# Feed-forward stages by seven block products: another order of units and products, sums beside the hi parts, a lent raw buffer

## The chip, the cores and the metric

The kernel runs on one core of one Trainium2 chip. The metric is the device time of one execution in microseconds, the median of several runs. TensorE is the engine of the matmuls, VectorE (DVE) and ScalarE (ACT) work on tiles in SBUF and in the banks of PSUM, SyncE (SP) issues the DMAs of the weights in order, GpSimd (POOL) does little here.

## What is computed

Two transformer blocks in float32 on 512 rows of 1024 columns. Of the whole, these lines of the reference are the part that the change touches, three feed-forward stages (two SwiGLU, one with a squared ReLU):

```python
def swiglu(x, w_in, w_out):
    gate, up = jnp.split(x @ w_in, 2, axis=-1)
    return (jax.nn.silu(gate) * up) @ w_out
...
        f = rmsnorm(h, pre_ff_g[l]) @ w_ff1[l]
        f = jnp.square(jax.nn.relu(f)) @ w_ff2[l]
```

`w_in` is 1024 x 5632 (22 blocks of 128 gate columns and 22 of 128 up columns), `w_ff1` 1024 x 4096. Attention, the mixers and the second matrices of the feed-forward stages stand between and are untouched.

## The kernel before

Every float32 product is made of three matmuls: each operand is split into a hi part, rounded to the type that TensorE takes in one pass, and a lo part, the remainder; `passes` (line 281) adds hi x hi, lo x hi and hi x lo. The activations stand transposed in `xh` and `xl` (8 blocks of 128 columns x 512 rows).

The weights come through the class `Weights`. `specs` lists the loads in order, each a tile of 128 x 1024 in one of three raw buffers (pool `raw`, name `wraw`); `load` (line 66) issues the next DMA on SP's queue. `units` lists what TensorE consumes, in order; `_split` (line 106) makes of a unit a hi part (`whi`, ScalarE, line 120) and a lo part (`wlo`, VectorE, line 121) in one of five pairs of buffers. `done` (line 148) tells that TensorE has read a unit; then `fill` splits the unit five places on, and `_loads` issues loads while raw buffers are free. A raw buffer is free when its last reader, a lo part, is done.

A feed-forward stage goes over pairs of column blocks, f = 0 to 21 in the first two (gate block f and up block f), 0 to 15 in the third. Pairs that are not in `FAST` (or `FAST1`) take two ordinary units, each 24 matmuls of 512 columns. A fast pair (`Blocks.__call__`, line 485) uses the scheme of seven block products instead of eight: the two weight tiles are four blocks, a11 and a12 (first column block, upper and lower half of the 1024 inputs), a21 and a22 (second column block), and x has four blocks as well, half of the inputs times half of the rows. Seven products of sums of blocks, each of 12 matmuls of 256 columns, 84 in all, are combined to four results. The sums of x stand in `th` and `tl`, made once in a stage by `steps` (two after each of the first ordinary tiles); those of the weights are made for each pair by four vector instructions in `_source` (lines 97 to 100), in the raw tiles themselves. A fast pair has four units:

- part 0: the first raw tile as it is (a11, a12), two products with x itself;
- part 1: a22 alone, half a tile, one product with a sum of x;
- part 2: the first tile after the four sums, a product with a sum of x and one with x;
- part 3: the second tile after the sums, two products with sums of x.

The products go to the two halves of four PSUM banks a, b, c, d; line 500 (ScalarE) and lines 506, 512, 513 and 514 (VectorE) add them up to `z`, from which the stage's activation is made (lines 784 and 785 in the first two stages). `z` and its helper `u` alternate between two places, one of which is a tile of its own.

The instructions of each engine but SP are put into an order by a scheduler when the program is built; SP's stand as the program calls them. Each engine works through its own in that order.

Of the kernel before, what the change touches and what calls it, by code (L numbers as in the profile page):

```python
# [10 lines left out]
F32 = mybir.dt.float32  # L11
# [44 lines left out]
class Weights:  # L56


    def __init__(self, nc, raw, pairs, specs, units, n_raw, n_pairs):
        self.nc, self.raw, self.pairs, self.specs, self.units = nc, raw, pairs, specs, units  # L60
        self.n_raw, self.n_pairs = n_raw, n_pairs
        self.loaded, self.used, self.split, self.released = 0, 0, 0, 0
        self.r, self.p, self.extra = {}, {}, set()

    def load(self, parts=0):
        i = self.loaded
        src, (a, b), n = self.specs[i]
        t = self.raw.tile([128, 1024], F32, name="wraw")
# [5 lines left out]
        self.loaded += 1  # L74
        if parts:
# [3 lines left out]

    def _source(self, i, part):  # L80

# [4 lines left out]
        if part is None:  # L86
            self.used += 1
            return self.r.pop(i)[:, :]
        if part == 0:
            return self.r[i][:, :]  # L90
        one, two = (self.r[i + n] for n in range(2))
        (a11, a12), (a21, a22) = ((t[:, :512], t[:, 512:]) for t in (one, two))
        if part == 1:
            return a22
        if part == 2:
            tt = self.nc.vector.tensor_tensor
            tt(a22, a21, a22, op=OP.add)  # L97
            tt(a21, a11, a21, op=OP.subtract)  # L98
            tt(a11, a22, a11, op=OP.subtract)  # L99
            tt(a12, a12, a11, op=OP.subtract)  # L100
            return one[:, :]
        self.used += 2
        del self.r[i], self.r[i + 1]
        return two[:, :]

    def _split(self, pool, steps=1, name=None):
        i, part = self.units[self.split]
        t = self._source(i, part)
# [8 lines left out]
        def step(steps):  # L117
            for s in steps:
                sl = slice(s * n, (s + 1) * n)
                self.nc.scalar.activation(hi[:, sl], t[:, sl], AF.Copy)  # L120
                self.nc.vector.tensor_tensor(lo[:, sl], t[:, sl], hi[:, sl].bitcast(F32), op=OP.subtract)  # L121
# [7 lines left out]
    def _loads(self):  # L129
        while self.loaded < min(self.used + self.n_raw, len(self.specs)):  # L130
            self.load()
# [27 lines left out]
def body(ctx, tc, ins, out, stop=None, dbg=None):  # L159
# [11 lines left out]
    specs, units, at = [], [], {}  # L171
# [7 lines left out]
    def spec_pair(key, w, c0, c1, fast):  # L179
# [5 lines left out]
        for m, c in enumerate((c0, c1)):  # L185
# [62 lines left out]
    W = Weights(nc, raw, pairs, specs, units, 3, 5)  # L248
# [203 lines left out]
    class Blocks:  # L452
# [29 lines left out]
        def __call__(self, key):  # L482
# [16 lines left out]
            product(0, 0, d[:, 0], X, 0, 0)  # L499
            nc.scalar.activation(z[:, 1], d[:, 0], AF.Copy)  # L500
            product(0, 1, a[:, 0], X, 1, 0)
            W.done(at[key, 0])
            product(1, 0, c[:, 1], T, 1, 0)
            W.done(at[key, 1])
            product(2, 0, a[:, 1], T, 1, 1)
            tt(z[:, 0:4:3], a, z[:, 1:2].to_broadcast([128, 2, 256]), op=OP.add)
            product(2, 1, c[:, 0], X, 1, 1)
# [834 lines left out]
```

## Time and profile before

| what | before |
|---|---|
| runs | 1786.63, 1788.59, 1794.02 us, median 1788.59 |
| profiled execution | 1788.74 us, its span 1787.0 us |
| TensorE busy (matmuls) | 1739.1 us, 97% |
| weight loads of TensorE busy | 1532.7 us, 86% |
| VectorE busy | 1184.7 us, 66% |
| ScalarE busy | 865.3 us, 48% |
| moved by DMA | 176.83 MB, 99 GB/s |

The span is the time from the first to the last instruction; the execution's own time is a little longer. Busy time of matmuls counts each from its start to its modelled end, and they overlap, so that it says little of what TensorE loses; starts do.

### The profile page before, as it was taken

Reading aid. Unit: us, or ns where it says so; the run is one execution under the profiler, and the core shown is the slowest. Engines: PE = TensorE matmul, PEld = TensorE weight load, DVE = VectorE, ACT = ScalarE, POOL = GpSimd, SP = SyncE. Lnnn points to the kernel's source line nnn. Section 1 sums busy time; section 2 is a strip of 40 time slices with the busy share of each in tenths; the row PEclk is TensorE's granted clock in tenths of the full one; section 3 lists DMA queues with packets and bytes.
Section 4 is the critical chain, followed back from the end, with each engine's and each line's share of the span. In section 5 each row is a group of like instructions: output and inputs, shape, how many; then the busy total and the mean of one; then the engine's idle time right before and its main releaser. Section 6 shows DMA issues by size and latency. Waiting matters only on the chain.

```text
span 1787.0 us, 26502 instructions
## 1 busy us (share of the span) xinstructions
PE 1739.1 (97%) x10496; PEld 1532.7 (86%) x10496; DVE 1184.7 (66%) x2028; ACT 865.3 (48%) x1470; POOL 70.9 (4%) x125
## 2 busy tenths in 40 slices
PE   8899999999999999999999999999999999999998
PEld 8788879899988888888899998888877899988886
DVE  6888856788764467777778878447456587773333
ACT  6878833334343258878443334233434444552232
POOL 0000002000000010000000000001101100000000
PEclk9999999999999999999999999999999999999999
DMA  6221236243353142322324244441322222343331
GB/s 204 59 60 60 83 100 196 76 114 95 95 171 124 48 125 83 90 83 71 107 60 114 78 116 124 137 131 48 96 82 77 83 83 82 108 142 107 100 100 47
DMA packets 198235, 176.83 MB, mean 99 GB/s; under 512 B 7008, under 2 KB 175136, under 8 KB 198112
## 3 DMA queue, kind: packets, MB, share of 16 engines
q1 hardware_dynamic: 194384, 162.48, 30.6%
q0 software_dynamic: 3152, 10.84, 2.1%
q8 instruction: 82, 1.34, 0.3%
q10 hardware_dynamic: 576, 1.84, 0.3%
q14 instruction: 41, 0.34, 0.1%
HBM read 172.99 MB, written 7.38 MB: 101 GB/s over the span
## 4 chain that ended last, share of the span: by engine, by line
PE 71%; DVE 12%; ACT 8%; DMA 6%; issue 2%; POOL 0%; ACTq 0%; SPq 0%; DVEq 0%; POOLq 0%
PE ps L286 35%; PE ps L372 30%; DMA wraw<-in_ffn_w_in 4%; ACT whi L120 4%; DVE wlo L121 3%; DMA wraw<-in_w_ff 1%; PE ps L302 1%; DVE wraw L100 1%; DVE wraw L98 1%; DVE wraw L99 1%; PE ps L884 1%; DVE wraw L97 1%; PE ps L872 1%; ACT x L616 1%; PE ps L571 1%
## 5 line engine op out<-in xcount | busy, mean ns | idle before, releaser
L120 ACT ACTIVATE whi<-wraw 128x1024 fp32r<-128x1024 f32 (+2 forms) x356 | 348.7, 1000 | 398.3 <-DVE wraw L100 133.6
L121 DVE TENSOR_TENSOR wlo<-wraw,whi 128x1024 fp32r<-128x1024 f32 (+2 forms) x356 | 405.4, 1155 | 189.1 <-ACT whi L120 187.0
L286 PE MATMUL ps<-xh,whi 128*128 128x256 f32 (+1 forms) x1260 | 406.6, 324 | 1.0 <-ACT xh L304 1.0
L286 PE MATMUL ps<-xl,whi 128*128 128x256 f32 (+1 forms) x1260 | 405.3, 322 | 0.5 <-DVE xl L305 0.3
L286 PE MATMUL ps<-xh,wlo 128*128 128x256 f32 (+1 forms) x1260 | 405.5, 322 | 0.0
L286 PEld LDWEIGHTS ps<-xh,whi 128*128 128x128 f32 x1260 | 238.5, 190 | 18.9 <-ACT xh L304 2.4
L286 PEld LDWEIGHTS ps<-xl,whi 128*128 128x128 f32 x1260 | 239.5, 190 | 17.2 <-DVE xl L305 1.0
L286 PEld LDWEIGHTS ps<-xh,wlo 128*128 128x128 f32 x1260 | 239.4, 190 | 17.2
L286 PE MATMUL ps<-th,wlo 128*128 128x256 f32 x624 | 175.0, 280 | 9.6 <-DVE wlo L121 9.4
L286 PE MATMUL ps<-th,whi 128*128 128x256 f32 x624 | 174.8, 280 | 8.3 <-ACT whi L120 8.3
L372 PE MATMUL ps<-whi,sh 128*128 128x512 f32 x568 | 175.8, 390 | 0.0
L372 PE MATMUL ps<-wlo,sh 128*128 128x512 f32 x568 | 175.6, 389 | 0.0
L372 PE MATMUL ps<-whi,sl 128*128 128x512 f32 x568 | 175.5, 389 | 0.0
L286 PE MATMUL ps<-tl,whi 128*128 128x256 f32 x624 | 173.3, 278 | 0.0
L754 DVE TENSOR_TENSOR sl<-h,sh 128x512 fp32r<-128x512 f32 x76 | 51.6, 691 | 175.5 <-ACT sh L753 175.5
L753 ACT ACTIVATE sh<-h 128x512 fp32r<-128x512 f32 x76 | 46.7, 628 | 212.9 <-PE ps L372 189.7
L286 PEld LDWEIGHTS ps<-th,wlo 128*128 128x128 f32 x624 | 117.8, 189 | 12.9 <-DVE wlo L121 12.8
L286 PEld LDWEIGHTS ps<-th,whi 128*128 128x128 f32 x624 | 117.9, 189 | 10.5 <-ACT whi L120 10.5
L286 PE MATMUL ps<-whi,xh 128*128 128x256 f32 (+1 forms) x384 | 125.8, 328 | 0.0
L372 PEld LDWEIGHTS ps<-whi,sl 128*128 128x128 f32 x568 | 106.6, 188 | 22.2
L372 PEld LDWEIGHTS ps<-wlo,sh 128*128 128x128 f32 x568 | 106.6, 188 | 22.2
L372 PEld LDWEIGHTS ps<-whi,sh 128*128 128x128 f32 x568 | 106.3, 188 | 21.8
(323 smaller groups left out, 2800.9 us busy)
## 6 DMA issues: line engine op xcount, KB each, us to landing
wraw<-in_ffn_w_in SPq DMA_DIRECT2D x88, 512.0 KB, 4.9
wraw<-in_w_ff SPq DMA_DIRECT2D x64, 512.0 KB, 4.0
wraw<-in_ffn_w_out SPq DMA_DIRECT2D x44, 512.0 KB, 3.5
wraw<-in_a_w_qkv SPq DMA_DIRECT2D x23, 512.0 KB, 4.0
wraw<-in_w_in SPq DMA_DIRECT2D x20, 512.0 KB, 3.7
wraw<-in_kv_w SPq DMA_DIRECT2D x16, 512.0 KB, 3.9
copies<-extd POOLq DMA_DIRECT2D x16, 320.0 KB, 8.5
wraw<-in_a_w_o SPq DMA_DIRECT2D x8, 512.0 KB, 3.5
```

The lines of the kernel that those rows point to most:

```text
L97: tt(a22, a21, a22, op=OP.add)
L98: tt(a21, a11, a21, op=OP.subtract)
L99: tt(a11, a22, a11, op=OP.subtract)
L100: tt(a12, a12, a11, op=OP.subtract)
L120: self.nc.scalar.activation(hi[:, sl], t[:, sl], AF.Copy)
L121: self.nc.vector.tensor_tensor(lo[:, sl], t[:, sl], hi[:, sl].bitcast(F32), op=OP.subtract)
L286: nc.tensor.matmul(ps, lhs[a][lsel], rhs[b][rsel], start=first and n == 0, stop=last and n == 2)
L302: nc.tensor.transpose(p[:, k, :], y[:, ts(4 * c + k)], ident)
L372: nc.tensor.matmul(self.banks[t][c], act[a][:, ts(t)], w[b][:, 0, c * 512:(c + 1) * 512], start=first and n == 0, stop=last and n == 2)
L571: yield lambda: nc.tensor.matmul(p[:, :N], part[m][:, ts(i)], part[2 + m][:, :N], start=True, stop=False)
L753: nc.scalar.activation(hi, src[k], AF.Copy)
L754: nc.vector.tensor_tensor(lo, src[k], hi.bitcast(F32), op=OP.subtract)
```

## The change

The two tiles of a fast pair are loaded in the other order, the second column block first. The units are: part 0 a22 alone; part 1 the other tile as it is; part 2 the tile of a21 and a22 after the first two sums; part 3 the tile of a11 and a12 after the other two, which are issued between the hi and the lo part of part 2 (`more`). The products follow the units. The raw tile of the second block is given back at part 2, that of the first at part 3. A set `lent` names loads, from f = 7 on, whose place in the list is divisible by four: they go into a tile that the stage lends (`room`, or the second `y` tile in the third stage) and that counts apart from the three raw buffers. The second `z` now lies in a free half of a tile of the stage.

```diff
--- before.py
+++ after.py
@@ -56,56 +56,62 @@
 class Weights:
 
 
-    def __init__(self, nc, raw, pairs, specs, units, n_raw, n_pairs):
-        self.nc, self.raw, self.pairs, self.specs, self.units = nc, raw, pairs, specs, units
-        self.n_raw, self.n_pairs = n_raw, n_pairs
-        self.loaded, self.used, self.split, self.released = 0, 0, 0, 0
+    def __init__(self, nc, raw, pairs, specs, units, lent, n_raw, n_pairs):
+        self.nc, self.raw, self.pairs, self.specs, self.units, self.lent = nc, raw, pairs, specs, units, lent
+        self.room, self.n_pairs, self.lender = [n_raw, 1], n_pairs, None
+        self.loaded, self.split, self.released = 0, 0, 0
         self.r, self.p, self.extra = {}, {}, set()
 
     def load(self, parts=0):
         i = self.loaded
         src, (a, b), n = self.specs[i]
-        t = self.raw.tile([128, 1024], F32, name="wraw")
+
+        t = self.lender() if i in self.lent else self.raw.tile([128, 1024], F32, name="wraw")
         v = t[:, :a * b].rearrange("p (a b) -> p a b", a=a)
         if n is not None:
             self.nc.gpsimd.memset(t[:, :a * b], 0.0)
             v = v[:, :, :n]
         self.r[i] = t
         self.loaded += 1
+        self.room[i in self.lent] -= 1
         if parts:
             part = lambda a, m: a[:, m * a.shape[1] // parts:(m + 1) * a.shape[1] // parts]
             return lambda m: self.nc.sync.dma_start(part(v, m), part(src, m))
         self.nc.sync.dma_start(v, src)
 
+    def _used(self, i):
+        self.room[i in self.lent] += 1
+        return self.r.pop(i)
+
     def _source(self, i, part):
+
 
 
 
         while self.loaded <= i + (part not in (None, 0)):
             self.load()
         if part is None:
-            self.used += 1
-            return self.r.pop(i)[:, :]
+            return self._used(i)[:, :], None
         if part == 0:
-            return self.r[i][:, :]
-        one, two = (self.r[i + n] for n in range(2))
-        (a11, a12), (a21, a22) = ((t[:, :512], t[:, 512:]) for t in (one, two))
+            return self.r[i][:, 512:], None
         if part == 1:
-            return a22
-        if part == 2:
-            tt = self.nc.vector.tensor_tensor
-            tt(a22, a21, a22, op=OP.add)
-            tt(a21, a11, a21, op=OP.subtract)
+            return self.r[i + 1][:, :], None
+        if part == 3:
+            return self._used(i + 1)[:, :], None
+        (a11, a12), (a21, a22) = ((t[:, :512], t[:, 512:]) for t in (self.r[i + 1], self.r[i]))
+        tt = self.nc.vector.tensor_tensor
+        tt(a22, a21, a22, op=OP.add)
+        tt(a21, a11, a21, op=OP.subtract)
+
+        def more():
             tt(a11, a22, a11, op=OP.subtract)
             tt(a12, a12, a11, op=OP.subtract)
-            return one[:, :]
-        self.used += 2
-        del self.r[i], self.r[i + 1]
-        return two[:, :]
+
+        return self._used(i)[:, :], more
 
     def _split(self, pool, steps=1, name=None):
         i, part = self.units[self.split]
-        t = self._source(i, part)
+        t, between = self._source(i, part)
         (a, b) = (t.shape[1] // 128, 128) if part is not None else self.specs[i][1]
         if name:
             both = pool.tile([128, 2048], F32, name=name).bitcast(F32R)
@@ -118,6 +124,8 @@
             for s in steps:
                 sl = slice(s * n, (s + 1) * n)
                 self.nc.scalar.activation(hi[:, sl], t[:, sl], AF.Copy)
+                if between:
+                    between()
                 self.nc.vector.tensor_tensor(lo[:, sl], t[:, sl], hi[:, sl].bitcast(F32), op=OP.subtract)
 
         step(range((steps + 1) // 2))
@@ -127,7 +135,7 @@
         return rest
 
     def _loads(self):
-        while self.loaded < min(self.used + self.n_raw, len(self.specs)):
+        while self.loaded < len(self.specs) and self.room[self.loaded in self.lent]:
             self.load()
 
     def ahead(self, pool, n, name=None):
@@ -168,7 +176,7 @@
         return bass.AP(tensor=w.tensor, offset=w.offset + r0 * ld + c0, ap=[[ld, 128], [128 * ld, nk], [1, n]])
 
 
-    specs, units, at = [], [], {}
+    specs, units, lent, at = [], [], set(), {}
 
     def spec(key, w, r0, nk, c0, n, pad=None, unit=True):
         if unit:
@@ -182,7 +190,9 @@
             for part in range(4):
                 at[key, part] = len(units)
                 units.append((len(specs), part))
-        for m, c in enumerate((c0, c1)):
+        for m, c in ((1, c1), (0, c0)) if fast else ((0, c0), (1, c1)):
+            if fast and key[-1] >= 7 and len(specs) % 4 == 0:
+                lent.add(len(specs))
             spec((key, "one", m), w, 0, 8, c, 128, unit=not fast)
 
     def rows(key, w, n):
@@ -245,7 +255,7 @@
     x = [const.tile([128, D], F32, name=f"x{t}") for t in range(NT)]
     xh = const.tile([128, KT, S], F32R, name="xh")
     xl = const.tile([128, KT, S], F32R, name="xl")
-    W = Weights(nc, raw, pairs, specs, units, 3, 5)
+    W = Weights(nc, raw, pairs, specs, units, lent, 3, 5)
 
     def load_x(t):
         nc.sync.dma_start(x[t], ins["x"][0, ts(t), :])
@@ -496,22 +506,22 @@
                            (*sel, slice(256 * right, 256 * right + 256)))
 
             X, T, tt = (xh, xl), self.t, nc.vector.tensor_tensor
-            product(0, 0, d[:, 0], X, 0, 0)
+            product(0, 0, c[:, 1], T, 1, 0)
+            W.done(at[key, 0])
+            product(1, 0, d[:, 0], X, 0, 0)
             nc.scalar.activation(z[:, 1], d[:, 0], AF.Copy)
-            product(0, 1, a[:, 0], X, 1, 0)
-            W.done(at[key, 0])
-            product(1, 0, c[:, 1], T, 1, 0)
+            product(1, 1, a[:, 0], X, 1, 0)
             W.done(at[key, 1])
-            product(2, 0, a[:, 1], T, 1, 1)
+            product(2, 0, b[:, 1], T, 0, 1)
+            product(2, 1, b[:, 0], T, 0, 0)
+            W.done(at[key, 2])
+            product(3, 0, a[:, 1], T, 1, 1)
             tt(z[:, 0:4:3], a, z[:, 1:2].to_broadcast([128, 2, 256]), op=OP.add)
-            product(2, 1, c[:, 0], X, 1, 1)
-            W.done(at[key, 2])
-            product(3, 0, b[:, 1], T, 0, 1)
-            product(3, 1, b[:, 0], T, 0, 0)
+            tt(u, b, z[:, 3:4].to_broadcast([128, 2, 256]), op=OP.add)
+            tt(z[:, 3], b[:, 0], u[:, 1], op=OP.add)
+            product(3, 1, c[:, 0], X, 1, 1)
             W.done(at[key, 3])
-            tt(u, b, z[:, 3:4].to_broadcast([128, 2, 256]), op=OP.add)
             tt(z[:, 1:3], c, u, op=OP.add)
-            tt(z[:, 3], b[:, 0], u[:, 1], op=OP.add)
             return z
 
     def part_project(key, state, part):
@@ -770,7 +780,9 @@
                 th, tl = (bp.tile([128, PAD + 8 * S], F32R, name=n)[:, PAD:].rearrange("p (j k s) -> p j k s", j=2, k=4)
                           for n, PAD in (("th", 112), ("tl", 0)))
                 blocks = Blocks([t.rearrange("p (k s) -> p k s", k=4) for t in four[4:6]], th, tl,
-                                lambda: bp.tile([128, 2 * S], F32, name="z"))
+                                lambda: four[5][:, 2 * S:])
+                room = bp.tile([128, 2 * S], F32, name="room")
+                W.lender = lambda: room
 
                 def evac(n, p):
                     f = n // 2
@@ -1279,6 +1291,14 @@
     with tc.tile_pool(name="blocks2", bufs=1) as bp:
         th, tl = (bp.tile([128, PAD + 8 * S], F32R, name=n)[:, PAD:].rearrange("p (j k s) -> p j k s", j=2, k=4)
                   for n, PAD in (("th2", 112), ("tl2", 0)))
+        room = []
+
+        def lender():
+            if not room:
+                room.append(yp.tile([128, D], F32, name="y"))
+            return room[0]
+
+        W.lender = lender
         blocks = Blocks([h[:, 14:18], h[:, 18:22]], th, tl, lambda: yp.tile([128, D], F32, name="y"))
         in_tiles(f1(0, 14), evac_f1, 5,
                  [[], [lambda: after_mix(2)], [], [], [lambda: after_mix(3)]], fast_f1, side_steps(blocks.steps(), 0, 2))
```

How the order of the instructions moves is seen at two places; line numbers are those of each kernel's own text. The first is VectorE in the first feed-forward stage, one round of the queue between fast pairs. L121 (now L129) makes a lo part, L97 to L100 (now L103, L104, L107, L108) the sums of the weights, L506 and L512 to L514 (now L519 to L521 and L524) the sums of the products, L785 (now L797) the result. Before:

```order
L121 TENSOR_TENSOR wlo<-wraw,whi 128x512
L785 TENSOR_TENSOR h_2789<-z 128x512
L97 TENSOR_TENSOR wraw<-wraw 128x512
L506 TENSOR_TENSOR gb<-ps,gb 128x2x256
L98 TENSOR_TENSOR wraw<-wraw 128x512
L99 TENSOR_TENSOR wraw<-wraw 128x512
L100 TENSOR_TENSOR wraw<-wraw 128x512
L121 TENSOR_TENSOR wlo<-wraw,whi 128x1024 x3
L512 TENSOR_TENSOR gb<-ps,gb 128x512
L513 TENSOR_TENSOR gb<-ps,gb 128x512
L514 TENSOR_TENSOR gb<-ps,gb 128x256
```

With the change:

```order
L519 TENSOR_TENSOR gb<-ps,gb 128x2x256
L520 TENSOR_TENSOR gb<-ps,gb 128x512
L129 TENSOR_TENSOR wlo<-room,whi 128x512
L521 TENSOR_TENSOR gb<-ps,gb 128x256
L524 TENSOR_TENSOR gb<-ps,gb 128x512
L103 TENSOR_TENSOR room<-room 128x512
L129 TENSOR_TENSOR wlo<-wraw,whi 128x1024
L797 TENSOR_TENSOR h_2789<-gb 128x512
L104 TENSOR_TENSOR room<-wraw,room 128x512
L107 TENSOR_TENSOR wraw<-room,wraw 128x512
L108 TENSOR_TENSOR wraw<-wraw 128x512
L129 TENSOR_TENSOR wlo<-room,whi 128x1024
```

All four sums stood before the three whole lo parts (parts 2 and 3, and part 0 of the next pair). Now the lo part of the half tile (512) comes first, that of part 1 stands between the first sum and the second, and the two last sums stand right before the lo part of part 2; that of part 3 (from `wraw`) follows behind the last row shown. Three of the sums of products stand ahead of or beside the half tile.

This is one of eight such runs of pairs; the others change alike.

The second is SP's queue from the end of the first attention into the first feed-forward stage. Before:

```order
L251 DMA x_77<-in_x 128x1024
L251 DMA x_78<-in_x 128x1024
L251 DMA x_79<-in_x 128x1024
L78 DMA wraw<-in_ffn_w_in 128x8x128 x41
L78 DMA wraw<-in_ffn_w_out 128x1024 x8
L292 DMA gb<-in_ln_g 128x1024
```

With the change:

```order
L261 DMA x_77<-in_x 128x1024
L261 DMA x_78<-in_x 128x1024
L261 DMA x_79<-in_x 128x1024
L80 DMA wraw<-in_ffn_w_in 128x8x128 x13
L80 DMA room<-in_ffn_w_in 128x8x128
L80 DMA wraw<-in_ffn_w_in 128x8x128 x3
```

From the fourteenth on, one of four loads now goes into `room`; nothing else on this queue changes its place. The queue of GpSimd is the same in both.

## Rows read from the trace of the kernel before

**Rows 1.** The page: span, and busy time with its share and instructions.
```profile
span 1787.0 us, 26502 instructions
...
PE 1739.1 (97%) x10496; PEld 1532.7 (86%) x10496; DVE 1184.7 (66%) x2028; ACT 865.3 (48%) x1470; POOL 70.9 (4%) x125
```

**Rows 2.** The timeline of TensorE round a stall: start us, us, engine, line, what [idle before].
```profile
971.51 0.28 PE L286 MATMUL ps<-tl,whi 128*128 128x256 f32 x1
971.62 0.28 PE L286 MATMUL ps<-th,wlo 128*128 128x256 f32 x1
972.67 0.39 PE L286 MATMUL ps<-th,whi 128*128 128x256 f32 x1 [0.77 <-ACT whi L120]
972.90 0.28 PE L286 MATMUL ps<-tl,whi 128*128 128x256 f32 x1
973.93 0.39 PE L286 MATMUL ps<-th,wlo 128*128 128x256 f32 x1 [0.76 <-DVE wlo L121]
```

**Rows 3.** The waits of the weight loads: engine, line, releaser: us in total, times, longest.
```profile
PEld ps L286 <- DVE wlo L121: 12.8, 16, 1.0
PEld ps L286 <- ACT whi L120: 10.5, 11, 2.3
```

**Rows 4.** The timeline of TensorE: first matmuls of four fast pairs, and a stall.
```profile
316.39 0.28 PE L286 MATMUL ps<-xh,whi 128*128 128x256 f32 x1
...
928.14 0.28 PE L286 MATMUL ps<-xh,whi 128*128 128x256 f32 x1
...
947.67 0.28 PE L286 MATMUL ps<-xh,whi 128*128 128x256 f32 x1
...
957.43 0.28 PE L286 MATMUL ps<-xh,whi 128*128 128x256 f32 x1
...
962.08 0.38 PE L286 MATMUL ps<-th,wlo 128*128 128x256 f32 x1
```

**Rows 5.** The timeline of SP's queue: two issues of weight loads.
```profile
950.17 0.37 SPq L78 DMA_DIRECT2D wraw<-in_ffn_w_in  x1
...
962.05 0.37 SPq L78 DMA_DIRECT2D wraw<-in_ffn_w_in  x1
```

**Rows 6.** The timeline of ScalarE in the same pair.
```profile
954.40 0.63 ACT L120 ACTIVATE whi<-wraw 128x512 fp32r<-128x512 f32 x1 [3.35 <-DMA wraw<-in_ffn_w_in]
...
959.70 2.96 ACT L120 ACTIVATE whi<-wraw 128x1024 fp32r<-128x1024 f32 x3 [4.15 <-DVE wraw L100]
```

**Rows 7.** The timeline of VectorE in the same pair.
```profile
955.06 0.69 DVE L121 TENSOR_TENSOR wlo<-wraw,whi 128x512 fp32r<-128x512 f32 x1 [0.99 <-ACT whi L120]
...
956.28 0.68 DVE L97 TENSOR_TENSOR wraw<-wraw 128x512 f32<-128x512 f32 x1
...
957.48 0.68 DVE L98 TENSOR_TENSOR wraw<-wraw 128x512 f32<-128x512 f32 x1
958.20 0.69 DVE L99 TENSOR_TENSOR wraw<-wraw 128x512 f32<-128x512 f32 x1
958.92 0.69 DVE L100 TENSOR_TENSOR wraw<-wraw 128x512 f32<-128x512 f32 x1
960.80 3.50 DVE L121 TENSOR_TENSOR wlo<-wraw,whi 128x1024 fp32r<-128x1024 f32 x3 [1.19 <-ACT whi L120]
```

**Rows 8.** Busy time by stretch: fast pairs of block two, and slow matmuls.
```profile
core 0: us, PE busy (x) PEld busy (x) DVE busy (x) ACT busy (x) POOL busy (x), PEclk, DMA share, GB/s
...
928.10:1118.00 189.90, 182.79 (x1406) 174.68 (x1406) 152.66 (x204) 78.97 (x107) 0.00 (x0) 1.00 0.37 106
...
355.30:358.60 3.30, 3.29 (x16) 3.29 (x17) 3.27 (x4) 0.86 (x2) 0.00 (x0) 0.53 0.64 168
```

**Rows 9.** The timeline of VectorE before the first fast pair.
```profile
313.19 1.22 DVE L475 TENSOR_TENSOR tl<-h,th 128x1024 fp32r<-128x1024 f32 x1
```

**Rows 10.** The page: issues of this weight's loads, KB each, median us to landing.
```profile
wraw<-in_ffn_w_in SPq DMA_DIRECT2D x88, 512.0 KB, 4.9
```

**Rows 11.** The chain that ended last: start us, us, what.
```profile
1039.89 6.36 DMA wraw<-in_ffn_w_in
```

## The prediction

> **What bounds the kernel now.** Read the page first. TensorE is busy 97% of the span and VectorE 66% [rows 1]; so only what TensorE loses can be won. A busy matmul says little here, since matmuls overlap: one of 256 columns lasts 0.28 us but the next starts 0.11 us later [rows 2]. So the second view is who the weight loads wait for. Two releasers matter: the vector instruction that makes a weight's lo part (line 121), 12.8 us in 16 waits, and the scalar one that makes its hi part (line 120), 10.5 us in 11 [rows 3]. All 27 lie in the runs of fast pairs: eight runs, three in each of the first two feed-forward blocks (f 4 to 8, 10 to 14, 16 to 20) and two in the third (4 to 8, 10 to 13), 39 pairs.
>
> Third, the timeline round one stall [rows 2]: the hi part comes at 972.67, where 971.73 would have done, and two matmuls later the lo part at 973.93. The first matmul after each wait takes 0.23 us instead of 0.11. Fourth, why the weights are late. A pair without a stall takes TensorE 957.43 - 947.67 = 9.76 us [rows 4], 84 matmuls, 0.116 each. The supply goes round in a longer circle. A raw buffer is released when the lo part of unit 2 is done, and SP issues the load at 950.17 [rows 5]. The hi part of the half tile starts at 954.40, released by that DMA [rows 6], its lo part at 955.06, the four sums stand from 956.28 to 959.6, the hi part of the first whole tile starts at 959.70 and its lo part at 960.80 [rows 6, 7]; 1.25 us later the next load is issued, at 962.05 [rows 5]. The circle takes 11.88 us, 2.12 more than TensorE's pair. Five units of finished weights hide three such deficits (6.4 us: the run that begins at 928.14 first stalls at 962.08, in its fourth pair [rows 4]); what comes after is a stall.
>
> **What the stalls cost.** The rows of weight loads give 12.8 + 10.5 = 23.3 us. Each counts from the end of the load before, some 0.04 us more than the lateness of the matmul: minus 1.1. The slow matmul behind each wait adds 27 x 0.11 = 3.0. And once, after the two longest waits in succession, TensorE was granted 0.53 of its clock for 3.3 us, which is the level of 1.2 GHz, and did 16 matmuls there at about 0.21 us [rows 8]: 16 x 0.1 = 1.6. Together **26.8 us**, the most that this change can give; nothing else in it makes a matmul shorter, and their number stays.
> The Trainium skill (TensorE: Matmul & The Clock Gate, Part 1) says that activity releases the throttle and idleness brings it back. By that the 1.6 us go with the stalls; the trace agrees, since the stretch follows the stall. Were it not so, the time below would be 1.6 us longer.
>
> **The change, part by part.** *Order of loads and units.* The second column block is loaded first; unit 0 is its right half, unit 1 the whole first tile, units 2 and 3 come after the sums. The half tile no longer hangs on a load that was issued a moment ago. In pairs that borrow nothing the circle is now: lo part of unit 2 done, load of the next pair's first tile issued, its hi part 4.23 us later (950.17 to 954.40), lo part 1.10 behind (959.70 to 960.80), then on the vector queue in the order shown above: that lo part 1.14 (three take 3.50, the last alone 1.22 of it), the product of the pair before last 0.60, the second sum 0.72, the third 0.72, the fourth 0.72 (sums that hang together stand 0.72 apart, 957.48, 958.20, 958.92 [rows 7]), the lo part of unit 2 with 1.23. Sum **10.46 us**, against 11.88. The deficit against TensorE is 0.7 a pair; four steps of a run make 2.8, under the 6.4 that were hidden before. So no stall even here.
>
> *Hi parts beside the next sums.* Two of the four sums now stand between the scalar hi part of unit 2 and the vector lo part. Before, VectorE idled 1.19 us there and 0.99 before the half tile's lo part [rows 7]. The first idle is filled by two sums (1.4 us beside the 1.10 from a hi part's start to its lo part), the second loses its cause, since that tile was loaded a pair earlier. VectorE's work itself is 11.88 - 1.19 - 0.99 = 9.70 us a pair, the count of its instructions unchanged: 0.06 under TensorE's 9.76. So VectorE is all but full, and I keep 0 to 0.3 us of idle a pair (waits for the hi parts of units 2 and 3; three hi parts take 2.96 [rows 6], about 1 each, beside the 1.14 of a lo part). At 0.3 a run of five gathers 4 x 0.24 = 1 us, covered by the lead; without the lead it would be a stall of 1 us in each of eight runs.
>
> *The fourth raw buffer.* From f 7 on, 15 loads go into the lent tile, one of four where pairs follow each other. The circle then spans two pairs, 19.5 us of TensorE for a chain of 10.5. On SP's queue the lent load waits for the lo part of unit 2 two pairs before, and the load behind it for that of unit 3 of the same pair, one lo part later; so it holds nothing up. GpSimd's queue is not moved.
>
> *Order of products.* Unit 0 now needs the sums of x, where the unsummed x went first. At the first pair of a stage these must be ready 2.8 us earlier. In the first block the third lo part (line 475), the one it reads, runs from 313.19 to 314.41 [rows 9], and the pair starts at 316.39 [rows 4]: 2.0 us to spare. The last is read only by unit 3, 7 us into the pair. Cost nothing; if the loads before it came 3 us later, 1 us once.
>
> *Evacuations.* Three of four output sums (new lines 519 to 521) can run before the pair ends. But the first waits for the first product of unit 3, 1.4 + 2.8 + 2.8 + 1.4 = 8.4 us into the pair, and behind it on VectorE stand the lo part of unit 0 and all that the pair after next needs. The last lo part ahead of that wait belongs to unit 3 of the next pair and is read at 9.76 + 7.0 = 16.8 us; the first behind it, unit 0 of the pair after next, needs a buffer that comes free at 9.76 and is read at 19.5. Both are made some 8 us before they are read; so the wait uses up lead, not time, as long as idle and work together stay near 9.76.
>
> **Sum.** The profiled execution took 1788.74 us, its span 1787.0 and 1.7 around it; the median of the runs is 1788.59, 0.15 less. 1788.7 - 26.8 = 1761.9. I add 1 us for small waits at the head of runs: **1763 us**. Ends: nothing left and 2 us of scatter below, 1759; above, 1 us left in each run and a late first pair, 1772.
>
> **Rivals.** *Loads in flight lengthen each other.* The median load of this weight lands after 4.9 us, and one of three in flight took 6.36 [rows 10, 11]. With a landing of 6.36 the circle of the pairs that borrow nothing (the first run of each stage) is 12.6, 2.8 over TensorE: three steps 8.5, less 6.4, leave 2.1 us in three runs: 1763 + 6 = 1769; with the same in the borrowed pairs up to 1774. For: the fourth buffer lets a load start sooner. Against: the two loads of a pair are still 1.1 us apart, and the DMA engines are busy 37% [rows 8]. Chance 0.10.
> The Trainium skill (Trainium Kernel Development and Optimization, Key Constraints) says that all queues run on the same 16 DMA engines and interleave; that is this rival's mechanism, and the 6.36 us agree with it.
> *VectorE becomes the bound at the old pace.* If the idle of 2.2 us a pair only moves to other places (hi parts of units 1, 2 and 3), the pace stays at 11.9 and the time at 1788, or half of it at 1776. For: 9.70 of 9.76 leaves no room. Against: the order of the queue puts two sums into the one hole, and the other has lost its cause. Chance 0.09.
> *Slower: the output sums lock VectorE to TensorE.* The wait of the first output sum falls into each pair as idle before the splits. With idle I a pair the pace is 9.7 + I, a run loses 4 x (9.7 + I - 9.76) - 6.4. To be 9 us slower than before, eight runs must lose 36, 4.5 each: I = 2.8, more than all the idle of a pair now. At 3.3 a run loses 6.6, the time is 1762 + 53 = 1815. Against: with weights a pair ahead that wait is served when its turn comes. Chance 0.04.
>
> **How the numbers follow.** Forecast 0.77 (1759 to 1768), first rival 0.10, second 0.09, third 0.04. The range 1759 to 1774 takes in the forecast and the first rival. Half a percent, 9 us, is about what a measurement of this kernel tells from no change: faster than 1779.6 are the forecast, the first rival and a share of the second, 0.89; within it 0.07; slower 0.04.
>
> **What would show it.** The weight loads' waits for lines 120 and 121 (new 126 and 129) fall from 23.3 us to under 4; pairs stand 9.8 us apart through a whole run; VectorE's idle before lo parts goes from 2.2 us a pair to under 0.5; no stretch of half clock near 355. Wrong would be: the waits remain with lo parts as releaser (VectorE bound), or with DMA behind them (loads), or TensorE waits for line 485 at the first fast pair.

## The result, and the profile after

| | before | changed |
|---|---|---|
| median of the runs | 1789.26 us (1786.63 to 1794.02) | 1760.06 us (1759.81 to 1760.24, and one of 5082.35) |
| ratio, 95% interval | | 0.9833 [0.9807, 0.986] |
| span of the profiled execution | 1787.0 us | 1758.0 us |

The changed kernel is faster by 29 us. One of its four executions took 5082.35 us at full clock; nothing recorded tells why, and the ratio leaves it out. The page of the changed kernel, against [rows 1]:

```profile
span 1758.0 us, 26549 instructions
...
PE 1727.9 (98%) x10496; PEld 1527.2 (87%) x10496; DVE 1184.7 (67%) x2028; ACT 875.1 (50%) x1470; POOL 70.9 (4%) x125
```

The work is the same (10496 matmuls, 1184.7 us of VectorE); the span lost what TensorE had waited. Of the waits of the weight loads in [rows 3], 23.3 us, none is left. The one wait for a weight's hi part in this view lies outside the fast pairs, and the kernel before has it too (line 1084 there, 0.2 us):

```profile
PEld ps L1096 <- ACT whi L126: 0.2, 1, 0.2
```

The timeline of TensorE at the first matmul of unit 1 in four pairs that follow each other, in the place of [rows 4]:

```profile
930.49 0.28 PE L296 MATMUL ps<-xh,whi 128*128 128x256 f32 x1
...
940.25 0.28 PE L296 MATMUL ps<-xh,whi 128*128 128x256 f32 x1
...
950.01 0.28 PE L296 MATMUL ps<-xh,whi 128*128 128x256 f32 x1
...
959.77 0.28 PE L296 MATMUL ps<-xh,whi 128*128 128x256 f32 x1
```

They stand 9.76 us apart each time; in the kernel before the fourth pair of this run stalled. The same stretches as in [rows 8], by the windows of the changed kernel:

```profile
core 0: us, PE busy (x) PEld busy (x) DVE busy (x) ACT busy (x) POOL busy (x), PEclk, DMA share, GB/s
928.10:1118.00 189.90, 189.90 (x1388) 179.70 (x1387) 150.99 (x199) 82.82 (x106) 0.00 (x0) 1.00 0.39 115
355.30:358.60 3.30, 3.30 (x30) 3.30 (x30) 3.23 (x5) 1.95 (x3) 0.00 (x0) 1.00 0.70 189
```

TensorE is busy in every microsecond of the stretch, and no clock of 0.53 is left near 355. Set side by side matmul by matmul, the two traces drift apart by 13.8 us in the first block's stage, 10.4 in the second's and 2.6 in the third stage: 26.8 in the three.

The circle of the raw buffers, in a pair that borrows nothing: SP's queue, ScalarE and VectorE (timeline: start, duration, line, what, idle before).

```profile
324.62 0.37 SPq L80 DMA_DIRECT2D wraw<-in_ffn_w_in  x1
...
334.89 0.37 SPq L80 DMA_DIRECT2D wraw<-in_ffn_w_in  x1
```
```profile
328.75 1.07 ACT L126 ACTIVATE whi<-wraw 128x1024 fp32r<-128x1024 f32 x1 [3.59 <-DMA wraw<-in_ffn_w_in]
...
332.37 1.06 ACT L126 ACTIVATE whi<-wraw 128x1024 fp32r<-128x1024 f32 x1 [1.77 <-DVE wraw L104]
```
```profile
329.85 1.22 DVE L129 TENSOR_TENSOR wlo<-wraw,whi 128x1024 fp32r<-128x1024 f32 x1 [0.51 <-ACT whi L126]
330.99 0.69 DVE L797 TENSOR_TENSOR h<-gb 128x512 f32<-128x512 f32 x1
331.59 0.68 DVE L104 TENSOR_TENSOR wraw<-wraw 128x512 f32<-128x512 f32 x1
332.31 0.69 DVE L107 TENSOR_TENSOR wraw<-wraw 128x512 f32<-128x512 f32 x1
333.04 0.69 DVE L108 TENSOR_TENSOR wraw<-wraw 128x512 f32<-128x512 f32 x1
333.65 2.52 DVE L129 TENSOR_TENSOR wlo<-wraw,whi 128x1024 fp32r<-128x1024 f32 x2
```

From issue to issue 334.89 - 324.62 = 10.27 us. The hi part of unit 2 (332.37) runs beside the last two sums (332.31, 333.04), and its lo part follows them with no idle, where [rows 7] had 1.19. One idle is left, 0.51 before the lo part of unit 1, which waits for the load.

### The profile page after: what moved, and what is told of

Read it like the earlier page. It is cut to its first block, busy times and chain, and to the rows that moved or that the text cites. A ratio compares the mean times of both kernels' runs of the same rounds, so it can differ in the third digit from the quotient of the medians.

```text
span 1758.0 us, 26549 instructions
## 1 busy us (share of the span) xinstructions
PE 1727.9 (98%) x10496; PEld 1527.2 (87%) x10496; DVE 1184.7 (67%) x2028; ACT 875.1 (50%) x1470; POOL 70.9 (4%) x125
## 4 chain that ended last, share of the span: by engine, by line
PE 89%; ACT 6%; DVE 4%; issue 1%; DMA 0%; POOL 0%; SPq 0%; DVEq 0%; POOLq 0%; ACTq 0%
PE ps L296 52%; PE ps L382 30%; PE ps L896 1%; PE ps L312 1%; PE ps L884 1%; ACT whi L126 1%; ACT x L626 1%; PE ps L581 1%; PE ps L582 1%; ACT qk L573 1%; DVE wlo L129 1%; ACT qk L569 0%; PE ps L688 0%; ACT b_e L875 0%; PE ps L1096 0%
## 5 line engine op out<-in xcount | busy, mean ns | idle before, releaser
L126 ACT ACTIVATE whi<-wraw 128x1024 fp32r<-128x1024 f32 (+2 forms) x326 | 329.3, 1014 | 310.1 <-PE ps L296 183.7
L129 DVE TENSOR_TENSOR wlo<-wraw,whi 128x1024 fp32r<-128x1024 f32 (+2 forms) x326 | 379.9, 1168 | 133.9 <-ACT whi L126 132.2
L296 PEld LDWEIGHTS ps<-xh,whi 128*128 128x128 f32 x1260 | 238.5, 190 | 18.7 <-ACT xh L314 2.4
L296 PE MATMUL ps<-wlo,xh 128*128 128x256 f32 (+1 forms) x384 | 123.1, 321 | 0.0
L296 PE MATMUL ps<-whi,xl 128*128 128x256 f32 (+1 forms) x384 | 123.1, 321 | 0.0
```

Source lines behind the costliest of these rows:

```text
L296: nc.tensor.matmul(ps, lhs[a][lsel], rhs[b][rsel], start=first and n == 0, stop=last and n == 2)
```

## The experiments

Each was compared with the kernel before on the same chip and in the same batch (medians there 1791.3 us for experiments 1 to 4, 1789.8 for 5 to 8, 1790.3 for 9 to 12). The first four asked which part of the change does it.

**1. The lent buffer alone**: the changed kernel with the loads, units, sums and products in the old order.

```diff
-        for m, c in ((1, c1), (0, c0)) if fast else ((0, c0), (1, c1)):
+        for m, c in ((0, c0), (1, c1)):
...
-        if part == 0:
-            return self.r[i][:, 512:], None
+        if part == 0:
+            return self.r[i][:, :], None
+        if part == 1:
+            return a22, None
...
```

> The loads, units, products and sums stand as in the kernel before; the lent fourth buffer alone is kept (from f 7 on, one load in four). Theory A, the circle of the raw buffers: with four buffers a circle of 11.9 us spans two pairs, 19.5 us, so the stalls vanish from the runs that borrow and stay only in the first run of the first stage (f 6 and 7, 5 to 7 us before): waits of the weight loads for hi and lo parts 5 to 8 us instead of 23.3, time 1766 to 1769. Theory B, the order is what did it: the waits stay near 20 us, time 1782 or more.

Measured: 1768.75 us, ratio 0.987 [0.9853, 0.9886]. The waits of its weight loads:

```profile
PEld ps L295 <- ACT whi L125: 3.6, 2, 2.4
PEld ps L295 <- DVE wlo L128: 2.2, 3, 1.0
```

All of these 5.8 us lie in the first run of the first block, where the lent tile comes into use only at f 7. The buffer alone gives 22.6 us, where experiment 2 below gives 30.6 against the same runs of the kernel before. In the other seven runs the weight loads wait less than 0.1 us in all, as Theory A had it.

**2. The new order alone**, without the lent buffer.

```diff
-            if fast and key[-1] >= 7 and len(specs) % 4 == 0:
-                lent.add(len(specs))
```

> The changed kernel without the lent buffer: every load takes one of the three raw buffers. Theory A, the circle: with the new order it is 10.5 us, 0.7 over TensorE's pair, four steps of a run make 2.8 us and the lead hides 6.4: no waits for weights, time 1760 to 1762. Rival, the fourth buffer is what took the stalls away: the runs from f 10 on stall as before, waits of 10 us or more, time 1770 to 1780.

Measured: 1760.71 us, 0.9827 [0.9813, 0.9842], with no wait for a weight in the fast pairs. So the two parts are two remedies for one deficit, and in runs of five pairs the new order needs no fourth buffer.

**3. All four sums written ahead of the hi part**, without the lent buffer.

```diff
-        return self._used(i)[:, :], more
+        more()
+        return self._used(i)[:, :], None
```

> No lent buffer, and all four sums stand before the hi part of unit 2 again, so nothing is done between its hi and its lo part. Theory A, the circle: 10.5 + 1.1 = 11.6 us, 1.8 over a pair, four steps 7.2 less 6.4: 0.8 us a run, some 6 us in all, time 1764 to 1768; VectorE idles 1.1 us more a pair before lo parts. Rival, the place of the sums costs nothing because ScalarE has time: time as without the fourth buffer, 1760 to 1762.

Measured: 1760.99 us, 0.9831 [0.9816, 0.9845]: a miss. In its trace the hi part of unit 2 still starts right after the second sum and beside the last two: it needs no more than the first two, and the scheduler had given VectorE, ScalarE and TensorE the same rows as in experiment 2. The place in the text, the "sums beside the hi parts", is worth nothing by itself.

**4. The old order of the loads**: first column block first, units, sums and products as in the change, no lent buffer.

```diff
-        for m, c in ((1, c1), (0, c0)) if fast else ((0, c0), (1, c1)):
+        for m, c in ((0, c0), (1, c1)):
...
-            return self.r[i][:, 512:], None
+            return self.r[i + 1][:, 512:], None
...
```

> No lent buffer; units, sums and products are those of the change, but the first column block is loaded first again, so that the half tile of unit 0 lies in the load issued last, and that load waits for the lo part of unit 3. Theory A, the circle: load 4.2, half hi and lo 1.3, two output sums 1.0, sum 0.6, lo 1.1, product 0.6, three sums 2.2, lo 1.1, lo 1.2 = 13.4 us, 3.6 over a pair, four steps 14.6 less 6.4: 8 us a run, time 1810 to 1825, slower than the kernel before. Rival, the order of loads is indifferent since both tiles of a pair are loaded together: 1760 to 1766.

Measured: 1772.88 us, 0.9892 [0.9878, 0.9907]: slower than experiment 2 by 12, far less than expected.

```profile
PEld ps L295 <- DVE wlo L130: 6.1, 11, 0.9
PEld ps L295 <- ACT whi L127: 1.5, 2, 0.9
```

But for one of 0.14 us the waits lie in the first block, where its load issues stand 11.9, 12.7 and 11.0 us apart; in the second they stand 11.0 and 10.8 apart, over 9.76 but within the lead. The kind was right, the circle of 13.4 was priced too long: not all that VectorE does in a pair stands in series within it. Why the first block's circle is longer than the second's was settled in part only: in its longest pair (12.7 us, against 10.8 for the pair at the same place of the second block) the load landed 5.5 us after its issue, against 3.7 there, and these 1.8 us are the whole difference; that of the other pairs stays open.

**5. The summed tiles not swapped**: unit 2 is the tile of a11 and a12 again, which needs all four sums; loads and units 0 and 1 as in the change, no lent buffer. The products of units 2 and 3 follow their tiles (not shown below), and with them the output sums stand as in the kernel before.

```diff
         if part == 3:
-            return self._used(i + 1)[:, :], None
+            return self._used(i)[:, :], None
...
+        tt(a11, a22, a11, op=OP.subtract)
+        tt(a12, a12, a11, op=OP.subtract)
+        return self._used(i + 1)[:, :], None
...
```

> The changed kernel without the lent buffer, and with the summed tiles in the old order: unit 2 is the tile of a11 and a12 and so waits for all four sums, unit 3 the other; the loads and units 0 and 1 stay as in the change. Theory A (what matters is that unit 2 hangs on two sums only, the other two standing beside its hi part): the circle becomes 4.23 + 1.10 + 1.14 + 0.60 + 2.88 + 1.10 + 1.23 = 12.3 us, 2.5 over a pair, a run of five loses 4 x 2.5 - 6.4 = 3.6, eight runs 29: 1790; since such a circle was overpriced before, 1770 to 1792. Rival (the order of the loads alone does it): 1760 to 1763, no weight waits.

Measured: 1777.08 us, 0.9924 [0.9909, 0.9939], 16 us over experiment 2. The waits of the weight loads, ScalarE at unit 1, and VectorE from unit 1 to unit 2:

```profile
PEld ps L291 <- DVE wlo L126: 9.9, 12, 1.0
PEld ps L291 <- ACT whi L123: 3.7, 6, 0.9
```
```profile
346.75 1.06 ACT L123 ACTIVATE whi<-wraw 128x1024 fp32r<-128x1024 f32 x1 [4.67 <-DMA wraw<-in_ffn_w_in]
```
```profile
347.84 1.23 DVE L126 TENSOR_TENSOR wlo<-wraw,whi 128x1024 fp32r<-128x1024 f32 x1 [0.42 <-ACT whi L123]
...
350.19 0.68 DVE L511 TENSOR_TENSOR gb<-ps,gb 128x512 f32<-128x512 f32 x1
350.79 0.68 DVE L106 TENSOR_TENSOR wraw<-wraw 128x512 f32<-128x512 f32 x1
352.65 2.96 DVE L126 TENSOR_TENSOR wlo<-wraw,whi 128x1024 fp32r<-128x1024 f32 x3 [1.18 <-ACT whi L123]
```

The idle of 1.18 us between the last sum and the lo part is back, as in [rows 7]. In the first block's first run the load issues stand 12.6, 12.0 and 10.9 us apart. In the pair shown (12.02, issued at 341.89) 1.75 us come on top of the 10.27 of the changed kernel: 1.0 between the two lo parts (the idle and an output sum, line 511, less a sum of the weights that now stands earlier) and 0.7 before the hi part of unit 1, which waits for its load. The idle is the part that experiment 3 had left untouched; what the moved output sum costs by itself no run shows.

The next runs tested the arithmetic of circle and lead with longer runs of fast pairs.

**6. The kernel before with longer runs.**

```diff
-FAST = (4, 5, 6, 7, 8, 10, 11, 12, 13, 14, 16, 17, 18, 19, 20)
-FAST1 = (4, 5, 6, 7, 8, 10, 11, 12, 13)
+FAST = tuple(range(4, 22))
+FAST1 = tuple(range(4, 14))
```

> The kernel before with the same longer runs, nothing else. Theory A (old circle of 11.88 us, 2.12 over a pair of TensorE, lead 6.4 us, refilled only by ordinary pairs): 17 x 2.12 - 6.4 = 29.6 us lost in each of the two long runs, 9 x 2.12 - 6.4 = 12.7 in the third, 72 together against 27 now, less 8 for the seven pairs that became shorter: 37 us slower than the kernel before, about 1827 (1815 to 1840). Rival (a stall belongs to the start of a run, some 3 us in each, whatever its length): three starts instead of eight, 1791 - 8 - 16 = 1767.

Measured: 1830.4 us, 1.0228 [1.0211, 1.0245]. The sum was right, its parts were not. The waits of its matmuls:

```profile
PE ps L286 <- DVE wlo L121: 26.8, 37, 0.8
PE ps L372 <- ACT sh L753: 16.2, 2, 8.4
PE ps L286 <- ACT whi L120: 9.7, 14, 1.6
```

Set side by side with experiment 7, which has the same matmuls and no stall in its runs, the three runs lost 23.8, 23.1 and 8.5 us, 55 of the 72 expected; 36.5 of them stand above as waits, each counted from the modelled end of the matmul before; the rest is what those ends hide, and slow matmuls behind the waits. In the first block the issues stand 11.8 us apart over the first five pairs and 11.0 in the rest, so the circle closes up in a long run; why, no run shows. The balance came from the two seams (line 372, the first products of the second matrix), 16.2 us in two waits and 19 with the slow matmuls behind them, which no step of the expectation had. In that part the total was right by luck.

**7. The changed kernel with the longer runs.** The same two lines.

> The changed kernel with every pair from f 4 on fast (18 in a row in the first two blocks, 10 in the third, where runs of five stood). Seven ordinary pairs of 10.92 us become fast ones of 9.76. Theory A (with the lent buffer the load's way is hidden, and the supply's pace is VectorE's work, 9.7 us a pair, so it holds for any length of run): no stall, 7 x 1.16 = 8.1 us less, 1752 (1750 to 1755). Rival B (the measured circle of 10.3 us sets the pace of the borrowed pairs too, and the ordinary pairs between the runs are what refills the lead of 6.4 us): 17 x 0.54 = 9.2, less 6.4, 2.8 us lost in each of the two long runs, 1757 to 1760, with waits of weight loads in the second half of a run.

Measured: 1753.36 us, 0.9798 [0.9783, 0.9813]. The windows of its first block:

```profile
384.00:470.00 86.00, 86.00 (x743) 86.00 (x742) 84.48 (x117) 40.34 (x54) 0.00 (x0) 1.00 0.39 111
```

TensorE never waits in this stretch, and VectorE is busy 84.48 of 86.00 us. SP's queue in the same stretch:

```profile
393.36 0.37 SPq L80 DMA_DIRECT2D room<-in_ffn_w_in  x1
...
403.05 0.37 SPq L80 DMA_DIRECT2D wraw<-in_ffn_w_in  x1
...
412.74 0.37 SPq L80 DMA_DIRECT2D room<-in_ffn_w_in  x1
```

The supply runs at 9.69 us a pair, just under TensorE's 9.76, and VectorE works 0.98 of that, 9.5 us, with 0.17 of idle. Theory A holds for the runs, and by these rows VectorE would be the next bound, which no run tests. Of the 8.1 us expected 6.7 came: at the seam of the first block TensorE now waits 0.45 and 0.75 us for the activation's hi and lo parts, where the changed kernel has no such wait.

**8. The longer runs without the lent buffer.**

> The same longer runs without the lent buffer. Theory A (a circle of 10.2 to 10.5 us against 9.76, a lead of 6.4 us): 17 x 0.44 to 0.74 = 7.5 to 12.6, less 6.4, 1 to 6 us lost in each of the two long runs, nothing in the third: 1755 to 1765, and the first wait not before the ninth pair. Rival (the circle shortens itself when TensorE comes near, since the scheduled order gives way): 1752, as with the lent buffer. If it is 1752, the fourth buffer is worth nothing in either form.

Measured: 1773.69 us, 0.9912 [0.9898, 0.9927], above the range. The first stall of the runs (timeline of TensorE, the idle before it in brackets):

```profile
417.55 0.38 PE L294 MATMUL ps<-th,wlo 128*128 128x256 f32 x1 [0.25 <-DVE wlo L129]
```

That is the eleventh pair. From there eight stalls lose 3.9 us in the first block's run and four lose 2.4 in the second's, side by side with experiment 7 (3.0 and 2.0 by the waits of the weight loads), as Theory A had it (1 to 6 each; the load issues stand 10.1 to 10.5 us apart). The rest was not foreseen. At the end of the first block's run, ScalarE and then TensorE:

```profile
496.81 1.06 ACT L126 ACTIVATE whi<-wraw 128x1024 fp32r<-128x1024 f32 x1 [2.00 <-DMA wraw<-in_ffn_w_out]
498.10 1.06 ACT L126 ACTIVATE whi<-wraw 128x1024 fp32r<-128x1024 f32 x1 [0.23 <-DMA wraw<-in_ffn_w_out]
499.06 1.66 ACT L761 ACTIVATE sh<-h 128x512 fp32r<-128x512 f32 x3
```
```profile
499.72 1.22 PE L380 MATMUL ps<-whi,sh 128*128 128x512 f32 x2 [4.92 <-ACT sh L761]
```
```profile
499.00:505.00 6.00, 5.28 (x13) 3.86 (x14) 5.94 (x10) 4.25 (x9) 0.00 (x0) 0.56 0.56 180
```

The activation's hi part (`sh`) stands on ScalarE's queue behind two hi parts of weights that wait for late loads. The first matmul of the second matrix waits 4.9 us (4.0 in the second block; 5.1 and 4.2 by the weight loads), and the stretch around it was granted 0.56 of the clock. With the slow matmuls behind them the two seams cost 5.7 and 6.7 us more than in experiment 7, the runs and seams of the two blocks together 18.7; the spans differ by 19.4.

**9. The same, with the last pair (f 21) ordinary.**

```diff
-FAST = tuple(range(4, 22))
+FAST = tuple(range(4, 21))
```

> Longer runs without the lent buffer, as before, but the last pair (f 21) of the first two blocks is ordinary again. There the longer runs lost 3 and 2 us to late weights, and 5.1 and 4.2 us more, with half-clock matmuls behind, where the second matrix begins. Theory A (the supply is late by the length of the run; at the seam the activation's hi part stands behind a weight's hi part on ScalarE's queue that waits for its load, so the lateness is paid a second time; an ordinary pair at the end gives the supply time): 1753.4 + 2.3 for the two pairs + 1.5 less at the seam, and 3 to 5 in the runs: 1757 to 1761. Rival (the seam costs this whatever stands before it, once the run is long): 1773 to 1776.

Measured: 1762.23 us, 0.9841 [0.9827, 0.9854], 1.2 over the range. Nothing waits at the seam any more; nine waits for lo parts are left in the runs, 3.4 us by the matmuls. So the seam took its loss from a supply that was already late, and an ordinary pair before it lets the supply catch up.

**10, 11. The changed kernel and the longer runs once more, on one chip.**

> The changed kernel once more, beside the longer runs on the same chip: 1759.5 to 1761, no waits for weights.

> The longer runs with the lent buffer once more, beside the changed kernel on the same chip. If what was measured holds, 1752.5 to 1754.5 and 6 to 7 us under the changed kernel; if it was a difference of the chips, the same as the changed kernel within 2 us.

Measured: 1760.99 us (1759.80 to 1761.05), 0.9832 [0.9819, 0.9846], and 1754.08 us (1753.10 to 1754.75), 0.9796 [0.9783, 0.981]: 6.9 us apart, and their runs don't overlap. The longer runs with the lent buffer beat both kernels.

**12. The longer runs begun at f 3.**

```diff
-FAST = tuple(range(4, 22))
+FAST = tuple(range(3, 22))
```

> The longer runs with the lent buffer, begun at f 3 in the first two blocks, one pair earlier. Theory A (the sums of x, which the first product of a fast pair now needs, are ready 2.0 us before the pair at f 4 starts; begun one pair earlier, their last steps are made beside a shorter time of TensorE, and TensorE waits for them): 2.3 us less for the two pairs, 2 to 12 us of waiting for the sums of x in each block, 1755 to 1770. Rival (they move up with the pair): 1751.

Measured: 1757.5 us, 0.9815 [0.9802, 0.9829], 3.4 over experiment 11. TensorE at the first fast pair, and ScalarE:

```profile
303.53 0.39 PE L296 MATMUL ps<-xh,wlo 128*128 128x512 f32 x1
306.38 0.39 PE L296 MATMUL ps<-th,whi 128*128 128x256 f32 x1 [2.46 <-ACT th L484]
```
```profile
305.27 1.06 ACT L484 ACTIVATE th<-h 128x1024 fp32r<-128x1024 f32 x1 [0.86 <-DVE h L487]
```

The sums of x do not move up far enough with the pair: 2.6 us lost here and 2.7 in the second block, against 2.3 won in the two blocks together. Of the two starts tried, f 4 is the better with this order of products.

## Why the prediction was right, point by point

**The stalls, 26.8 us.** Shown: the two traces drift apart by 26.8 us in the three stages. The 1.6 us of half clock went with the stalls: near 355 the clock stayed at 1.00. In experiment 1, where the two waits at that place are left (2.17 and 0.61 us by the matmuls), so is the slow stretch: 0.50 was granted from 354.10 to 360.90. The Trainium skill (TensorE: Matmul & The Clock Gate, Part 1), cited in the prediction, says that idleness brings the throttle back; both traces agree here. But one reading of the prediction was wrong: the waits at the slow stretch (1.68 and 0.76 us by the matmuls) are not the two longest in succession. Those stand at the end of the same block's fast pairs, and no slow stretch follows them:

```profile
491.86 0.39 PE L286 MATMUL ps<-th,whi 128*128 128x256 f32 x1 [2.11 <-ACT whi L120]
...
493.12 0.38 PE L286 MATMUL ps<-th,wlo 128*128 128x256 f32 x1 [0.76 <-DVE wlo L121]
```
```profile
493.10:496.50 3.40, 3.38 (x29) 3.38 (x29) 3.17 (x4) 1.40 (x3) 0.00 (x0) 1.00 0.62 176
```

So the length of the waits alone does not tell where the clock falls. The forecast came out 3 us too long for two reasons. The 1 us that I added for waits at the heads of runs did not appear. And 2.0 us net went ahead of the first fast pair, which no step of mine named (last section). The medians differ by 29.2 us; whether each execution of the kernel before pays those 2.0 is not shown.

**The circle, 11.88 to 10.46.** Measured 10.27 in the pair shown above, 10.1 to 10.5 in experiments 2 and 8, which borrow nowhere. Its pieces: from issue to hi part 4.13 (4.23 predicted), to the lo part 1.10, that lo part and the product 1.14 and 0.60 as predicted, three sums 2.06 instead of 2.16, the last lo part 1.24. That a deficit adds up pair by pair until the lead is gone is borne out by experiment 8, and by the absence of any stall in five pairs in experiment 2; experiment 6 had the sign and the total, but not the parts. As a sum the rule is coarse. For the kernel before it gives 4 x 2.12 less 6.4, 2.1 us in a run of five, where side by side the eight runs lost between 1.2 and 7.1 us each: in the first run of the first block the issues stand 11.9, 12.8 and 11.6 us apart, and TensorE first waits in the third pair, not the fourth. The 26.8 us came from the rows of waits, not from circle and lead. What the theory lacked is that neither is a constant: the circle closed up from 11.8 to 11.0 in a long run (experiment 6), and experiments 4 and 5 cost 12 and 16 us where the circles I priced gave 50 or more, and 29.

**"Hi parts beside the next sums."** The idle of 1.19 us went, filled by the last two sums, as the step had it. What it left open is what lets them stand there. Not where they are written, which does nothing (experiment 3), but that unit 2 became the tile that needs two sums instead of four: with the old tile there, the idle came back, and the kernel was 16 us slower than experiment 2 (experiment 5, where an output sum moved as well). VectorE's work was put at 9.70 us a pair and measured 9.5; its idle at 0 to 0.3 and measured 0.17 (experiment 7).

**The fourth raw buffer.** That the circle then spans two pairs is right (experiments 1 and 7). It was not said that the new order makes it superfluous in runs of five (experiment 2). In runs of eighteen it is worth 20 us (experiments 7 and 8).

**The order of products, nothing lost.** Right, but with less room than 2.0 us: in the changed trace the third lo part of the sums of x starts at 312.23 and, at 1.22 us, ends 0.97 before the pair starts at 314.42. One pair earlier it costs 2.6 us (experiment 12).

**The evacuations.** Right: with VectorE 98% busy in experiment 7, TensorE waits nowhere in the run.

**The rivals.** In the median the loads did not land later: 4.4 us into the raw buffers and 4.0 into the lent tile, where [rows 10] had 4.9; single ones still took up to 6.4 into the lent tile, and nothing waited for them. VectorE did not become the bound at the old pace, and the output sums locked nothing. The lateness that appeared at the seam of the longer runs was none of the rivals.

## What to carry to other kernels

Price the circle of a buffer (released, issued, landed, split, released) against the time that the consumer needs for the same data, multiply the difference by the pairs in a row and subtract the lead: here that told which runs would stall, and the size of a stall only roughly. When the run ends late, look at what stands behind the waiting instruction at the seam, since the lateness can be paid there a second time. When two edits cure the same deficit, their gains don't add; spend the spare on something else (here longer runs of the cheaper pairs, 6.9 us more). And look for the cause in what an instruction depends on rather than where it is written: the scheduler had already moved the sums.

## What the runs showed of the hardware that was not expected

TensorE's clock after the same idle was not always the same. In attention, outside the change, TensorE waits 2.1 us for a vector instruction in both kernels. Before (timeline, then window):

```profile
140.01 0.45 PE L678 MATMUL ps<-ident,x 128*128 128x128 f32 x1 [2.10 <-DVE x L670]
```
```profile
139.00:143.00 4.00, 2.99 (x12) 3.02 (x13) 3.26 (x8) 3.87 (x10) 0.00 (x0) 0.62 0.00 0
```

And in the changed kernel:

```profile
139.36 0.30 PE L688 MATMUL ps<-ident,x 128*128 128x128 f32 x1 [2.09 <-DVE x L680]
```
```profile
139.00:143.00 4.00, 3.64 (x29) 3.67 (x30) 3.26 (x10) 3.85 (x9) 0.00 (x0) 1.00 0.00 0
```

Before, the matmuls behind the wait ran at 1.2 GHz until about 143 us (0.21 us apart instead of 0.12); in the changed kernel the clock stayed at 2.4 GHz. All fourteen profiles have this wait, 2.09 to 2.10 us long, at 139.4 to 141.1 us; two of them (the kernel before and experiment 5, where it ends at 140.01 and 140.02) show the slow stretch behind it, and experiment 8, where it ends at 140.00, does not. So neither the length of an idle nor its place decided, and what did these runs don't show.

The same two profiles stand apart from the others once before, after a wait of 2.92 to 2.93 us that all fourteen have, and that ends at 86.16 in the kernel before and at 86.78 in the changed kernel. The windows of the two kernels:

```profile
85.00:93.00 8.00, 6.84 (x32) 6.48 (x32) 7.90 (x20) 4.98 (x9) 0.00 (x0) 0.57 0.22 67
```
```profile
85.00:93.00 8.00, 6.21 (x37) 6.07 (x38) 7.91 (x20) 6.04 (x13) 0.00 (x0) 0.79 0.19 60
```

Both fall to 1.2 GHz here, the kernel before for longer. Experiment 5 was granted 0.57 in this window as well, the eleven other profiles 0.79. Side by side the kernel before loses 1.3 us at this place and 1.5 behind the wait at 140; the changed kernel loses 0.8 in its first 12 us. Up to the first fast pair that makes the 2.0 us of the result that belong to no part of the change; such a difference between two profiles should be looked for before a mechanism is made for it.
